# The projections' banks enter the scheduler's estimate, and the forget-gate decays reach the causal mask by accumulating DMA: a three-layer transformer kernel on one core

## The chip, the core and the metric

The kernel runs on one core of a Trainium2 chip. The metric is the time of one execution on the device, in microseconds (us). The engines are named as in the profile: PE is TensorE (matmuls, transposes), DVE VectorE, ACT ScalarE, POOL GpSimd, SP SyncE (it only issues transfers here). Each engine works through its own instructions strictly in program order and waits on semaphores for the others. SP and POOL also each own a queue of DMA transfers, which land asynchronously. DRAM is the device memory, SBUF the memory on the core, and a bank is one of eight accumulators of 128 x 512 f32 (PSUM) into which PE writes.

## What is computed

512 tokens of width 1024 go through three transformer layers in f32: block 1 once (block-sparse MoBA attention, gated linear attention GLA, a feed-forward network), then block 2 twice. The part of block 2 that the change touches, cut from the reference:

```python
log_f = jax.nn.log_sigmoid((f_logit + b_forget).astype(jnp.float32))
c = jnp.cumsum(log_f.astype(jnp.float32), axis=1).transpose(0, 2, 1)      # 8 heads
...
scores = jnp.einsum('bqhd,bkhd->bhqk', q_i, k).astype(jnp.float32) * scale
bias = c_i[..., :, None] - c[..., None, :]
causal = key_pos[None, :] <= q_pos[:, None]
logits = jnp.where(causal, scores + bias, -jnp.inf)
p = jax.nn.softmax(logits, axis=-1)
...
ret = retention_chunkwise(q_r, k_r, rv.reshape(rshape), gamma)
mixed = jnp.concatenate([fox_out.astype(x.dtype), ret_out], axis=-1)
x = layernorm(DEEPNORM_ALPHA * x + jnp.einsum('bsc,cd->bsd', mixed, w_out), ln1_g, ln1_b)
hid = jnp.square(jax.nn.relu(jnp.einsum('bsd,df->bsf', x, w_ff1)))
x = layernorm(DEEPNORM_ALPHA * x + jnp.einsum('bsf,fd->bsd', hid, w_ff2), ln2_g, ln2_b)
```

Attention has 8 heads of 64, handled as 4 pairs (pair 0 is heads 0 and 1, h0 and h1, and so on). Of the bias only the decay c at one of the two positions is added to the scores; the other is the same over a whole softmax row and drops out.

## The kernel before

**Precision.** Every f32 operand is split into a high and a low part in fp32r, and a product is three matmuls: high x high, low x high, high x low. Names with h or l at the end are the parts (wh, wl of a weight block; xTh, xTl of the activations; kh, kl of the keys).

**Weights.** A block of 512 KB is loaded by SP into `wr` (3 buffers), copied to `wh` by ACT (6 buffers), and DVE subtracts to get `wl`. The ACT copy waits until PE has finished with the block six back; SP's load waits for the DVE subtraction three back. All of this is issued in the order in which the program asks for blocks, mixed in each engine's queue with the attention's own work.

**Banks.** Four banks of tag "mm" take projections (`mm_ps`), four of tag "at" take everything else: scores, transposes, attention outputs (`at_ps`). Projections come in two forms. `proj_a` makes one 128-column slice for all tokens (24 matmuls into one bank): so q and k of each pair (q0, k0, ... q3, k3). `proj_b` takes all four mm banks for 512 columns: so the values. In block 2 the order is: values of attention, q0 k0 q1 k1 q2 k2 q3 k3, values of retention (a `proj_b`), then retention's own projections.

**Attention.** `attention_pair` turns the two banks of q and k into operands per head (ACT copies qs and kh, DVE makes the scaled qs and kl), which frees the banks. Then per head come the scores (8 matmuls in three banks), the softmax with its row maxima (DVE: instructions that add the bias, write ea, eb, ec and reduce; ACT: exponentials), transposes of the result (PE, tiles pta, ptb, ptc), and per pair the product with the values.

**What sets PE's order.** The program is a set of Python generators, threads, of which `Weave.run` advances one at a time while the kernel is built. Each instruction is charged to an estimate of its engine (`Engine.book`); `wv.now` is the estimated PE time. A thread that yields an event is not resumed before the event's estimated time, and one that yields a count is not resumed before that many "at" banks are free by the estimate (`banks`). So an estimate decides the order that every engine then follows, and a bad estimate costs a wait on the chip. The mm banks are not in it: a `proj_a` takes its bank at once, whether or not the chip will have freed it.

**The bias.** Block 2 writes the summed decays of the 8 heads to DRAM (`cd`). `fox_bias` loads one causal mask `tri` (128 x 512) per layer; per head SP loads that head's decays, the same 512 values for each of 128 partitions, into `row`, and POOL adds `cm` = `row` + `tri`. DVE uses `row` left of the diagonal blocks and `cm` on them. `row`, `tri` and `cm` come from a shared pool of 56 buffers of 256 KB.

Of the kernel before, what the change touches and what calls it, by code (L numbers as in the profile page):

```python
# [10 lines left out]
F32 = mybir.dt.float32  # L11
# [3 lines left out]
ALU = mybir.AluOpType  # L15
# [4 lines left out]
P, T, D = 128, 512, 1024  # L20
# [3 lines left out]
NM = 4  # L24
LAG = 0.6
SLACK = 0.0
HOLD = 1.5
BIG = 1.0e30
# [125 lines left out]
class Event:  # L154


    t = None


class Weave:  # L160
# [4 lines left out]
    def __init__(self, banks):  # L165
        self.now = self.chain = self.ready = 0.0
        self.threads, self.count = [], 0
        self.banks = {i: 0.0 for i in range(banks)}

    def spawn(self, gen, prio=1):  # L170
        self.count += 1
# [6 lines left out]
    def charge(self, eng, cost, args):  # L178
        self.chain = eng.book(self.chain, cost)
        self.ready = max(self.ready, self.chain)  # L180
        for a in args:
            n = getattr(getattr(a, "tensor", None), "name", None)
            if n in self.banks:
                self.banks[n] = max(self.banks[n], self.chain + HOLD)

    def bank(self, tile):

        del self.banks[min(self.banks, key=self.banks.get)]
        self.banks[tile.tensor.name] = self.now

    def mark(self, ev, more=0.0):
        ev.t = self.chain + LAG + more
# [75 lines left out]
def model_kernel(ctx: ExitStack, tc: tile.TileContext, I, out):  # L268
    nc = tc.nc
# [7 lines left out]
    psm = ctx.enter_context(tc.tile_pool(name="psm", bufs=NM, space=PSUM))  # L277
# [4 lines left out]
    wv = Weave(8 - NM)  # L282
    act, dve, pool = Engine(nc.scalar, wv, 0.2, 0.83), Engine(nc.vector, wv, 0.17, 1.04), Engine(nc.gpsimd, wv, 0.25, 2.1)
    uid = [0]

    def nm(s):
        uid[0] += 1
        return f"{s}_{uid[0]}"

    def bt(s="b", dt=F32):  # L290
        return pb.tile([P, T], dt, tag="b", name=nm(s))
# [7 lines left out]
        return pv.tile([P, 16], F32, tag="v", name=nm(s))  # L299

    def mm_ps():
        return psm.tile([P, T], F32, tag="mm", name=nm("mm"))

    def at_ps():
        t = psa.tile([P, T], F32, tag="at", name=nm("at"))
# [44 lines left out]
    def wblk(*key, pieces=1):  # L350
        key = key if len(key) == 7 else (*key, "")
        off, size = offs[key]
        nk = (key[3] - key[2]) // P
        raw = pw.tile([P, 1024], F32, tag="wr", name=nm("wr"), bufs=3)
        src = I["wall"][off : off + size].rearrange("(p w) -> p w", p=P)
        hi = pw.tile([P, 1024], F32R, tag="wh", name=nm("wh"))
        cuts = [slice(1024 // pieces * i, 1024 // pieces * (i + 1)) for i in range(pieces)]
        for c in cuts:
            with tc.issue_after(xdma[0].ins) if xdma else nullcontext():
                last_dma[0] = nc.sync.dma_start(raw[:, c], src[:, c])  # L360
            copy(hi[:, c], raw[:, c])
        if key[6]:
            h3 = hi.rearrange("p (k w) -> p k w", k=nk)
            r3 = raw.rearrange("p (k w) -> p k w", k=nk)
            sub_lo(h3[:, :, 32:64], r3[:, :, 32:64], h3[:, :, 32:64])
            return h3
        lo = pw.tile([P, 1024], F32R, tag="wl", name=nm("wl"))
        for c in cuts:
            sub_lo(lo[:, c], raw[:, c], hi[:, c])
        return hi.rearrange("p (k w) -> p k w", k=nk), lo.rearrange("p (k w) -> p k w", k=nk)  # L370
# [20 lines left out]
    def form_a(ps, w, c, acts, ks, toks=slice(0, T)):  # L391

        wh, wl = w
        n = len(ks)
        for i, k in enumerate(ks):
            h, l = acts.hs[k][:, toks], acts.ls[k][:, toks]
            mm(ps[:, toks], wh[:, i, c : c + P], h, i == 0, False)
            mm(ps[:, toks], wh[:, i, c : c + P], l, False, False)
            mm(ps[:, toks], wl[:, i, c : c + P], h, False, i == n - 1)
            yield 0  # L400
# [11 lines left out]
            yield 0  # L412

    def proj_a(name, l, c, acts, k=8):
        ps = mm_ps()
        yield from form_a(ps, wblk(name, l, 0, k * P, c, c + P), 0, acts, range(k))
        return ps

    def proj_b(name, l, k0, k1, c, acts, done, koff=0, tail=0, wait_k=False, wait_t=False, pre=None):
# [27 lines left out]
    def const(n):  # L447
        src = const_src(n)
        t = bt(n)[:, 0 : src.shape[1]]
        load(t, src)  # L450
        return t
# [48 lines left out]
    def row_bcast(src, n0):  # L500

        t = bt("row")
        load(t, bass.AP(tensor=src.tensor, offset=src.offset + n0, ap=[[0, P], [1, T]]))
        return t
# [686 lines left out]
        yield from block2(0, xw2, h)  # L1191


    def fox_bias(cd, tri):
        def bias(h):
            cb, cm = row_bcast(cd, T * h), bt("cm")
            pool.tensor_tensor(cm, cb, tri, ALU.add)

            def pieces(t):
                d = (P * t, P * t + P, cm[:, P * t : P * t + P])  # L1200
                return [d] if t == 0 else [(0, P * t, cb[:, 0 : P * t]), d]

            return pieces

        return bias
# [56 lines left out]
    def block2(l, xw, h):  # L1262
# [6 lines left out]
        dve.tensor_tensor_scan(a[0:8], one[0:8].to_broadcast([8, T]), f[0:8], 0.0, ALU.mult, ALU.add)  # L1269
        cd = pd.tile([8, T], F32, tag="cd", name=nm("cd"))  # L1270
        nc.sync.dma_start(cd, a[0:8])
        bias = fox_bias(cd, const("tri"))
        mix = Acts(8, "mix")
        for i in range(4):
            qk = []
# [16 lines left out]
        for i in range(4):  # L1292
            qk = []
            for j in range(2):
                ps = yield from proj_a("w_in_2", l, 1544 + 512 * j + P * i, xw)
# [9 lines left out]
        for i in range(4):  # L1305
            ps = yield from proj_a("w_in_2", l, 3080 + P * i, xw)
            ev, sg = sgs[i]
# [71 lines left out]
```

## Time and profile before

| quantity | value |
|---|---|
| time, median of 3 runs | 2039.48 us (2037.76 to 2041.69) |
| the profiled execution: time | 2039.07 us |
| its span (first to last instruction) | 2036.2 us |
| mean granted clock of PE, as a share of full speed | 0.993 |
| PE busy | 1990.4 us, 98% of the span |
| DVE, ACT, POOL busy | 56%, 47%, 16% |
| chain of work that ended last | 94% PE |

The span is the part of the time that the profile sees; 2.87 us of the profiled execution lie outside it. Idle time counts only on the engine that sets the end, and here that is PE. An idle stretch is shown in brackets behind the instruction that ended it, with the instruction that released it. The granted clock is what the chip's throttle let PE run at: 1.00 is 2.4 GHz and 0.50 is 1.2 GHz, the two levels; a value between is a mean over both.

### The profile page before, as it was taken

To read this page: it belongs to the slowest core of one execution; us is meant where nothing else is said; L and a number is where in the kernel's file an instruction comes from. 1 tells how busy PE (TensorE), PEld (TensorE's weight loads), DVE (VectorE), ACT (ScalarE), POOL (GpSimd) and SP (SyncE) were. 2 spreads that over 40 slices of the span, in tenths; PEclk is the share of its full clock that TensorE was granted. 3 is DMA by queue.
4 is the path that set the end of the run, shared out by engine and by line. 5 is a ranking of instruction groups with operands and counts; after the bars stand their busy time and mean duration, and the time that the engine had idled before them with its cause. 6 is when DMAs were issued, how large, how long until landed. Compare 5 with 4: busy or idle time off the path is not lost.

```text
span 2036.2 us, 25412 instructions
## 1 busy us (share of the span) xinstructions
PE 1990.4 (98%) x9478; PEld 1645.5 (81%) x9478; DVE 1148.5 (56%) x2028; ACT 954.0 (47%) x1663; POOL 319.1 (16%) x361
## 2 busy tenths in 40 slices
PE   8999899999999999999999999999999999999997
PEld 6777778888888888877888888888877888888886
DVE  6676444444566573475454656664675554656654
ACT  6566244333555453364333554552564334544551
POOL 2000110000212110010402201111211412211102
PEclk9999999999999999999999999999999999999999
DMA  5422112242766543332232745552422234666541
GB/s 200 156 91 76 52 63 93 94 154 73 181 158 137 154 126 114 100 108 80 81 125 92 167 144 130 150 149 79 140 84 87 69 115 142 138 159 157 131 133 42
DMA packets 93483, 240.49 MB, mean 118 GB/s; under 512 B 10734, under 2 KB 11200, under 8 KB 93360
## 3 DMA queue, kind: packets, MB, share of 16 engines
q1 hardware_dynamic: 72624, 201.12, 29.3%
q0 software_dynamic: 20736, 37.76, 11.6%
q8 instruction: 74, 1.21, 0.2%
q14 instruction: 49, 0.40, 0.1%
HBM read 236.69 MB, written 4.77 MB: 119 GB/s over the span
## 4 chain that ended last, share of the span: by engine, by line
PE 94%; ACT 2%; DVE 2%; POOL 1%; issue 1%; DMA 0%; SPq 0%; POOLq 0%; ACTq 0%; DVEq 0%
PE mm L311 67%; PE at L311 25%; PE at L320 3%; POOL h L262 1%; ACT wh L262 0%; ACT kh L262 0%; DMA xr<-in_xT_dram 0%; DVE og L262 0%; ACT qs L262 0%; DVE wl L262 0%; DVE qs L262 0%; ACT sil L262 0%; POOL mv L262 0%; ACT h L262 0%; POOL gm L262 0%
## 5 line engine op out<-in xcount | busy, mean ns | idle before, releaser
L262 DVE TENSOR_TENSOR wl<-wr,wh 128x1024 fp32r<-128x1024 f32 (+1 forms) x265 | 336.3, 1271 | 331.0 <-ACT wh L262 329.8
L262 ACT ACTIVATE wh<-wr 128x1024 fp32r<-128x1024 f32 (+1 forms) x268 | 282.5, 1056 | 474.4 <-PE mm L311 328.5
L262 DVE TENSOR_TENSOR wl<-sw,wh 128x512 fp32r<-128x512 f32 x252 | 166.0, 687 | 194.1 <-ACT wh L262 194.1
L262 ACT ACTIVATE wh<-sw 128x512 fp32r<-128x512 f32 x252 | 149.8, 626 | 224.9 <-PE at L311 121.6
L311 PE MATMUL at<-hTh,wh 128*128 128x512 f32 x576 | 224.1, 389 | 0.0
L311 PE MATMUL at<-hTl,wh 128*128 128x512 f32 x576 | 224.1, 389 | 0.0
L311 PE MATMUL at<-hTh,wl 128*128 128x512 f32 x576 | 224.1, 389 | 0.0
L669 POOL DMA_DIRECT2D sw<-in_wall_dram x144 | 127.3, 1051 | 606.7 <-DVE wl L262 450.1
L311 PE MATMUL mm<-xTh,wh 128*128 128x512 f32 x536 | 214.1, 399 | 0.0
L311 PE MATMUL mm<-xTl,wh 128*128 128x512 f32 x536 | 209.0, 390 | 0.0
L311 PE MATMUL mm<-xTh,wl 128*128 128x512 f32 x512 | 200.0, 391 | 0.0
L311 PE MATMUL mm<-wh,xl 128*128 128x512 f32 x504 | 196.2, 389 | 0.0
L311 PE MATMUL mm<-wl,xh 128*128 128x512 f32 x504 | 196.1, 389 | 0.0
L311 PE MATMUL mm<-wh,xh 128*128 128x512 f32 x504 | 196.1, 389 | 0.0
L311 PE MATMUL mm<-wh,xTh 128*128 128x512 f32 x352 | 146.2, 415 | 12.7 <-ACT wh L262 6.4
L311 PE MATMUL mm<-wl,xTh 128*128 128x512 f32 x352 | 140.0, 398 | 0.0
L311 PE MATMUL mm<-wh,xTl 128*128 128x512 f32 x352 | 139.7, 397 | 0.0
L311 PEld LDWEIGHTS at<-hTh,wh 128*128 128x128 f32 x576 | 108.2, 188 | 22.4
L311 PEld LDWEIGHTS at<-hTh,wl 128*128 128x128 f32 x576 | 108.1, 188 | 22.5
L311 PEld LDWEIGHTS at<-hTl,wh 128*128 128x128 f32 x576 | 108.1, 188 | 22.4
L311 PEld LDWEIGHTS mm<-xTh,wh 128*128 128x128 f32 x536 | 100.8, 188 | 19.6 <-ACT wh L262 0.5
L311 PEld LDWEIGHTS mm<-xTl,wh 128*128 128x128 f32 x536 | 100.9, 188 | 18.8
(287 smaller groups left out, 3809.6 us busy)
## 6 DMA issues: line engine op xcount, KB each, us to landing
wr<-in_wall_dram SPq DMA_DIRECT2D x266, 512.0 KB, 3.6
sw<-in_wall_dram SPq DMA_DIRECT2D x144, 256.0 KB, 5.8
sw<-in_wall_dram POOLq DMA_DIRECT2D x144, 256.0 KB, 6.0
row<-cd SPq DMA_DIRECT2D x16, 256.0 KB, 4.1
revp<-rev SPq DMA_DIRECT2D x1, 2560.0 KB
xr<-in_xT_dram SPq DMA_DIRECT2D x8, 256.0 KB, 6.1
g<-revp SPq DMA_DIRECT2D x8, 256.0 KB, 3.9
h<-in_x_dram SPq DMA_DIRECT2D x8, 256.0 KB, 5.9
```

The costliest lines, as they stand in the source:

```text
L262: return f(out, *a, **k)
L311: nc.tensor.matmul(out, lhsT, rhs, start=start, stop=stop, skip_group_check=more)
L320: nc.tensor.transpose(out, in_, ident)
L669: nc.gpsimd.dma_start(t, src, accum_op=ALU.add)
```

## The change

It has two parts. First, the estimate gets a second table, `mm`, for the four mm banks: a bank taken is marked as in use without end (BIG), and every charged instruction that touches it moves the time at which it comes free to its own end plus HOLD. `proj_a` now builds its weight block first, then yields `mm_free`, an event at the time when the first mm bank comes free by the estimate, and only then takes its bank. `proj_b` takes its four banks as before, with no yield. Second, `fox_bias` loads a fresh copy of `tri` for each head instead of one per layer, and adds the decays to it by a DMA on POOL's queue that accumulates into SBUF, straight from `cd`; the POOL addition and its charge in the estimate are gone. `row` is still loaded, for the blocks left of the diagonal.

```diff
     def __init__(self, banks):
 ...
         self.banks = {i: 0.0 for i in range(banks)}
+        self.mm = {i: 0.0 for i in range(NM)}
 ...
             if n in self.banks:
                 self.banks[n] = max(self.banks[n], self.chain + HOLD)
+            if n in self.mm:
+                self.mm[n] = self.chain + HOLD if self.mm[n] == BIG else max(self.mm[n], self.chain + HOLD)
 ...
+    def mm_bank(self, tile):
+
+        del self.mm[min(self.mm, key=self.mm.get)]
+        self.mm[tile.tensor.name] = BIG
+
+    def mm_free(self):
+
+        ev = Event()
+        t = min(self.mm.values())
+        ev.t = t if t < BIG else self.now
+        return ev
 ...
     def mm_ps():
-        return psm.tile([P, T], F32, tag="mm", name=nm("mm"))
+        t = psm.tile([P, T], F32, tag="mm", name=nm("mm"))
+        wv.mm_bank(t)
+        return t
 ...
     def proj_a(name, l, c, acts, k=8):
+        w = wblk(name, l, 0, k * P, c, c + P)
+        yield wv.mm_free()
         ps = mm_ps()
-        yield from form_a(ps, wblk(name, l, 0, k * P, c, c + P), 0, acts, range(k))
+        yield from form_a(ps, w, 0, acts, range(k))
         return ps
 ...
-    def fox_bias(cd, tri):
+    def fox_bias(cd):
         def bias(h):
-            cb, cm = row_bcast(cd, T * h), bt("cm")
-            pool.tensor_tensor(cm, cb, tri, ALU.add)
+            cb, cm = row_bcast(cd, T * h), const("tri")
+            nc.gpsimd.dma_start(cm, bass.AP(tensor=cd.tensor, offset=cd.offset + T * h, ap=[[0, P], [1, T]]), accum_op=ALU.add)
 ...
-        bias = fox_bias(cd, const("tri"))
+        bias = fox_bias(cd)
```

The number of instructions on PE, DVE, ACT and POOL stays the same; SP issues 14 more. The order differs in three stretches: block 1 from its attention to the end of GLA, and the attention of block 2 in each of its two layers (which change alike). Everything else, the feed-forward networks among it, is ordered as before.

**Block 2, layer 0, pair 3 on PE.** The names: `mm_1349` before and `mm_1367` after is the bank of k3; `mm_1372` before and `mm_1374` after is the first of the four banks of the `proj_b` behind it; `at<-kh,qs` are scores of head h4, in banks at_1368 and at_1370 before, at_1372 after. Before:

```order
L311 MATMUL at_1368_7328<-kh_1329_7166,qs_1328_7165 128x512
L311 MATMUL at_1368_7328<-kl_1330_7167,qs_1328_7165 128x512
L311 MATMUL at_1370_7337<-kh_1329_7166,qs_1328_7165 128x384
L311 MATMUL at_1370_7337<-kl_1330_7167,qs_1328_7165 128x384
L311 MATMUL mm_1349_7250<-xTh_736_3888,wh_1351_7252 128x512
L311 MATMUL mm_1349_7250<-xTl_738_3890,wh_1351_7252 128x512
L311 MATMUL mm_1349_7250<-xTh_736_3888,wl_1352_7255 128x512
```

After:

```order
L328 MATMUL mm_1367_7331<-xTh_737_3889,wh_1365_7326 128x512
L328 MATMUL mm_1367_7331<-xTl_739_3891,wh_1365_7326 128x512
L328 MATMUL mm_1367_7331<-xTh_737_3889,wl_1366_7329 128x512
L328 MATMUL at_1372_7365<-kh_1340_7220,qs_1339_7219 128x512
L328 MATMUL at_1372_7365<-kl_1341_7221,qs_1339_7219 128x512
L328 MATMUL mm_1367_7331<-xTh_737_3889,wh_1365_7326 128x512
L328 MATMUL mm_1367_7331<-xTl_739_3891,wh_1365_7326 128x512
L328 MATMUL mm_1367_7331<-xTh_737_3889,wl_1366_7329 128x512
L328 MATMUL mm_1374_7377<-wh_1379_7382,xTh_736_3888 128x512
L328 MATMUL mm_1374_7377<-wl_1380_7385,xTh_736_3888 128x512
L328 MATMUL mm_1374_7377<-wh_1379_7382,xTl_738_3890 128x512
```

Two banks of h4's scores stood ahead of 18 of k3's 24 matmuls; now the first stands among the last of them, and the rest come after matmuls of the `proj_b`.

**The same place on DVE.** `qs` and `kl` with a 64x512 tile are the operands of pair 3, which read the banks of q3 and k3 (`mm_1324`, `mm_1349` before; `mm_1338`, `mm_1367` after) and free them; the rows on `ea`, `eb` belong to h4's softmax. Before:

```order
L262 TENSOR_SCALAR ea_1340_7193<-ea_1340_7193,mx_1369_7331 128x512
L262 TENSOR_TENSOR wl_1479_7840<-wr_1477_7836,wh_1478_7837 128x1024
L262 RECIPROCAL mx_1371_7340<-mx_1371_7340 128x1
L262 COPY pta_1366_7326<-at_1379_7377 128x512
L262 TENSOR_SCALAR eb_1341_7194<-eb_1341_7194,mx_1371_7340 128x384
L262 SCALAR_TENSOR_TENSOR qs_1380_7383<-mm_1324_7155,qs_1380_7383 64x512
L262 TENSOR_TENSOR kl_1382_7385<-mm_1349_7250,kh_1381_7384 64x512
L262 SCALAR_TENSOR_TENSOR qs_1385_7396<-mm_1324_7155,qs_1385_7396 64x512
L262 TENSOR_TENSOR kl_1387_7398<-mm_1349_7250,kh_1386_7397 64x512
```

After:

```order
L277 ISA ea_1351_7249,mx_1373_7368<-at_1372_7365,row_1342_7228 128x384
L277 ISA mx_1373_7368 128x1
L277 SCALAR_TENSOR_TENSOR qs_1381_7390<-mm_1338_7215,qs_1381_7390 64x512
L277 ISA ea_1351_7249,mx_1373_7368<-at_1372_7365,tri_1343_7230,mx_1373_7368 128x128
L277 ISA mx_1373_7368 128x1
L277 TENSOR_TENSOR wl_1477_7845<-wr_1475_7841,wh_1476_7842 128x1024
L277 TENSOR_TENSOR kl_1383_7392<-mm_1367_7331,kh_1382_7391 64x512
L277 RECIPROCAL mx_1373_7368<-mx_1373_7368 128x1
L277 TENSOR_SCALAR ea_1351_7249<-ea_1351_7249,mx_1373_7368 128x512
L277 SCALAR_TENSOR_TENSOR qs_1386_7404<-mm_1338_7215,qs_1386_7404 64x512
L277 TENSOR_TENSOR kl_1388_7406<-mm_1367_7331,kh_1387_7405 64x512
```

The four operand rows stood behind all of h4's first reductions and a copy of transposes (`pta`); now only the reduction of h4's first bank stands among them.

**Block 1, pairs 2 and 3 on DVE.** `qs`, `kl` here are the operands of pair 2 and then of pair 3, from transposes in "at" banks; `ea_303<-at_327` (before `ea_302<-at_327`) is the first reduction of h4's scores, which frees the bank at_327. Before:

```order
L262 SCALAR_TENSOR_TENSOR qd_305_1428<-gqk_269_1290,qd_305_1428 128x512
L262 TENSOR_TENSOR ki_306_1429<-gqk_279_1341,ki_306_1429 128x512
L262 TENSOR_TENSOR yml_12_106<-at_309_1441,ymh_8_102 128x512
L262 SCALAR_TENSOR_TENSOR qs_315_1474<-at_313_1464,gains_97,qs_315_1474 64x512
L262 SCALAR_TENSOR_TENSOR kl_317_1476<-at_314_1465,gains_97,kh_316_1475 64x512
L262 SCALAR_TENSOR_TENSOR qs_319_1485<-at_313_1464,gains_97,qs_319_1485 64x512
L262 SCALAR_TENSOR_TENSOR kl_321_1487<-at_314_1465,gains_97,kh_320_1486 64x512
L262 ISA ea_302_1424,mx_328_1503<-at_327_1500,g_295_1409 128x512
```

After:

```order
L277 SCALAR_TENSOR_TENSOR qs_307_1441<-at_305_1431,gains_97,qs_307_1441 64x512
L277 SCALAR_TENSOR_TENSOR kl_309_1443<-at_306_1432,gains_97,kh_308_1442 64x512
L277 SCALAR_TENSOR_TENSOR qs_311_1452<-at_305_1431,gains_97,qs_311_1452 64x512
L277 SCALAR_TENSOR_TENSOR kl_313_1454<-at_306_1432,gains_97,kh_312_1453 64x512
L277 SCALAR_TENSOR_TENSOR qd_320_1469<-gqk_269_1290,qd_320_1469 128x512
L277 TENSOR_TENSOR ki_321_1470<-gqk_279_1341,ki_321_1470 128x512
L277 TENSOR_TENSOR wl_430_2017<-wr_428_2013,wh_429_2014 128x1024
L277 ISA ea_303_1429,mx_328_1509<-at_327_1506,g_296_1414 128x512
```

A weight subtraction (`wl_430`) now stands ahead of the reduction; it needs the ACT copy `wh_429`, which stands on ACT behind all operand copies of both pairs.

**Block 2, layer 0 on SP.** `cd` holds the decays, `wr` are weight blocks. Before:

```order
L360 DMA wr_1400_7458<-in_wall_dram 128x1024
L348 DMA row_1264_6900<-cd_1231_6799 128x512
L360 DMA wr_1423_7575<-in_wall_dram 128x1024
L348 DMA row_1269_6913<-cd_1231_6799 128x512
L360 DMA wr_1432_7629<-in_wall_dram 128x1024
L360 DMA wr_1467_7771<-in_wall_dram 128x1024
L348 DMA row_1299_7046<-cd_1231_6799 128x512
L348 DMA row_1304_7059<-cd_1231_6799 128x512
```

After:

```order
L365 DMA row_1263_6898<-cd_1231_6799 128x512
L365 DMA tri_1264_6900<-in_c128_dram 128x512
L377 DMA wr_1425_7590<-in_wall_dram 128x1024
L365 DMA row_1268_6912<-cd_1231_6799 128x512
L365 DMA tri_1269_6914<-in_c128_dram 128x512
L377 DMA wr_1449_7716<-in_wall_dram 128x1024
L377 DMA wr_1467_7788<-in_wall_dram 128x1024
L365 DMA row_1303_7064<-cd_1231_6799 128x512
L365 DMA tri_1304_7066<-in_c128_dram 128x512
L365 DMA row_1308_7078<-cd_1231_6799 128x512
L365 DMA tri_1309_7080<-in_c128_dram 128x512
```

Behind each `row` now stands a load of `tri`; on POOL each addition `cm<-row,tri` is replaced by a DMA `tri<-cd`, at the same place in its queue.

## Rows read from the trace of the kernel before

**Rows 1.** The page: busy time of the engines, and the chain that ended last

```profile
PE 1990.4 (98%) x9478; PEld 1645.5 (81%) x9478; DVE 1148.5 (56%) x2028; ACT 954.0 (47%) x1663; POOL 319.1 (16%) x361
...
PE 94%; ACT 2%; DVE 2%; POOL 1%; issue 1%; DMA 0%; SPq 0%; POOLq 0%; ACTq 0%; DVEq 0%
```

**Rows 2.** Waits of PE: for what, us in total, times, longest us

```profile
PE mm L311 <- DVE qs L262: 5.9, 2, 2.9
```

**Rows 3.** Timeline of PE, block 2 (idle before, releaser); both layers' attention

```profile
901.43 0.39 PE L311 MATMUL at<-kh,qs 128*128 128x256 f32 x1 [0.85 <-ACT pta L262]
...
918.57 0.49 PE L311 MATMUL mm<-wh,xTh 128*128 128x512 f32 x1 [2.94 <-DVE qs L262]
...
1517.36 0.79 PE L311 MATMUL mm<-wh,xTh 128*128 128x512 f32 x1 [2.94 <-DVE qs L262]
```

**Rows 4.** Stretches: length, busy us (instructions) of each engine, clock, DMA share, GB/s

```profile
918.50:922.00 3.50, 3.43 (x11) 2.72 (x12) 1.83 (x4) 1.07 (x2) 2.51 (x2) 0.61 0.02 9
922.00:926.00 4.00, 4.00 (x23) 3.25 (x22) 1.01 (x1) 2.42 (x4) 0.00 (x0) 0.91 0.00 0
1517.00:1521.00 4.00, 3.64 (x10) 2.86 (x11) 2.12 (x4) 1.32 (x3) 2.51 (x2) 0.50 0.10 35
1521.00:1525.00 4.00, 4.00 (x20) 3.25 (x18) 0.00 (x0) 1.68 (x3) 0.00 (x0) 0.69 0.00 0
220.00:224.00 4.00, 3.84 (x13) 3.15 (x14) 1.07 (x3) 0.19 (x1) 0.00 (x0) 0.63 0.00 0
250.00:260.00 10.00, 8.61 (x48) 6.92 (x48) 4.64 (x9) 2.51 (x4) 1.19 (x2) 1.00 0.29 91
```

**Rows 5.** Timeline of ACT, block 2, layer 0, pair 3

```profile
911.78 1.06 ACT L262 ACTIVATE wh<-wr 128x1024 fp32r<-128x1024 f32 x1 [0.43 <-PE mm L311]
...
913.35 0.57 ACT L262 ACTIVATE qs<-mm 64x512 fp32r<-64x512 f32 x1
```

**Rows 6.** Timeline of DVE, the same place

```profile
912.88 1.23 DVE L262 TENSOR_TENSOR wl<-wr,wh 128x1024 fp32r<-128x1024 f32 x1 [0.67 <-ACT wh L262]
...
917.82 0.69 DVE L262 SCALAR_TENSOR_TENSOR qs<-mm,qs 64x512 fp32r<-64x512 f32 x1 [1.30 <-ACT qs L262]
```

**Rows 7.** Tile row: count, ns min/median/max, first and last start; landing of its loads

```profile
L348 SPq DMA_DIRECT2D row<-cd x16: 370/384/427, 864.6 to 1513.8; - x16
L262 POOL TENSOR_TENSOR cm<-row,tri x16: 1274/1296/2256, 868.6 to 1518.9; 128x512 f32<-128x512 f32 x16
...
DMA to landing us min/median/max: 3.7/4.4/7.1
```

**Rows 8.** Timeline of DVE, first uses of cm: heads h0, h1, h2

```profile
876.39 0.34 DVE L262 CUSTOM_DVE_ANT_0 ea<-at,cm,mx 128x128 f32<-128x128 f32 x1
...
879.31 0.33 DVE L262 CUSTOM_DVE_ANT_0 ea<-at,cm,mx 128x128 f32<-128x128 f32 x1
...
902.87 0.35 DVE L262 CUSTOM_DVE_ANT_0 ea<-at,cm,mx 128x128 f32<-128x128 f32 x1
```

**Rows 9.** Timeline of SP's queue, loads of row for h0, h1, h2 and h3

```profile
864.63 0.37 SPq L348 DMA_DIRECT2D row<-cd  x1
...
869.45 0.42 SPq L348 DMA_DIRECT2D row<-cd  x1
...
882.45 0.90 SPq L348 DMA_DIRECT2D row<-cd  x2
```

**Rows 10.** Tile sw, weights of the FFNs: POOL's accumulating DMAs; landing of all

```profile
L669 POOL DMA_DIRECT2D sw<-in_wall_dram x144: 862/875/1870, 524.3 to 1936.0; - x144
...
DMA to landing us min/median/max: 3.6/5.9/10.1
```

**Rows 11.** Timeline of PE, block 1: the idle stretches where the order changes

```profile
158.90 0.36 PE L311 MATMUL at<-kh,qs 128*128 128x256 f32 x1 [1.94 <-DVE qs L262]
...
220.16 2.07 PE L311 MATMUL at<-v,kt 128*128 128x256 f32 x4 [4.13 <-DVE sta L262]
```

**Rows 12.** Timeline of ACT, block 1: the last operand copy of pair 3

```profile
160.15 0.63 ACT L262 ACTIVATE kl<-kl 64x512 fp32r<-64x512 f32 x1 [0.16 <-DVE kl L262]
```

## The prediction

> **What bounds the kernel now.** I read the page first: PE is busy for 98% of the span and makes up 94% of the chain that ended last [rows 1]. The work on PE is the same before and after, so only two things can move the time: PE's idle stretches, and the clock that PE is granted behind them. The view of PE's waits shows where a projection's bank was missing: two waits of 2.94 us, both on DVE's `qs` [rows 2]. The timeline places one in each layer of block 2. The stalled matmul is `mm<-wh,xTh`, which only a `proj_b` issues: it is the third of the four banks that the value projection of retention takes, and it was q3's. Another 0.85 us stands earlier in each layer, on a copy of transposes [rows 3].
>
> The windows show what a stall costs beyond itself. Behind the 2.94 us the clock is 0.61 for 3.5 us and 0.91 for 4 us in one layer, 0.50 and 0.69 for 4 us each in the other. Against 1.00 this loses 3.5 x 0.39 + 4 x 0.09 = 1.73 us and 4 x 0.50 + 4 x 0.31 = 3.24 us. The 4.13 us stall in block 1 has 0.63 for 4 us behind it, 1.48 us lost; an idle stretch of 1.39 us (inside 250 to 260 us) leaves the clock at 1.00 [rows 4]. So a short stall costs its length, a stall of 2.9 us or more costs 1.5 to 3.2 us on top. The Trainium skill, TensorE: Matmul & The Clock Gate, says that idle time on the engine drops its clock; these windows agree.
>
> Lost now in block 2's attention, per layer: 0.85 + 2.94 of stall, and 1.73 or 3.24 of clock: 5.5 and 7.0, together 12.5 us. This is what the change can win there.
>
> **Part one: the order, block 2.** After the change h4's scores follow most of k3's matmuls, so the operands of pair 3 no longer queue on DVE behind h4's softmax. Before, DVE reached the last `qs` of pair 3 at 917.82 us [rows 6], and PE stood until then. After, I chain by hand: k3's last matmuls end about 910.7; behind them ACT has a weight copy of 1.06 us and operand copies of 0.57 each [rows 5], DVE a `wl` of 1.23 and operand rows of 0.69 each [rows 6]. That puts the `qs` that frees q3's bank at 915.0 to 915.7. PE, with its shorter stalls, wants this bank at 914.5. So the wait does not vanish, since `proj_b` has no yield for its banks; it shrinks from 2.94 to about 1.25 us (0.5 to 2). The 0.85 us goes, because the copy of transposes now has projection matmuls between. I add 0.75 us for the biases (below) and 1 us for waits that I can't see, and take 3 us per layer, 2 at the least that I can chain. None is as long as 2.9 us, so the clock should stay. Gain in block 2: 12.5 - 2 x 3 = 6.5 us; 8.5 if only the chained 2 us remain.
>
> **Part one: block 1.** There the order moves too, though no projection waited for its mm bank. Gone are 0.19 + 1.94 = 2.13 us, of which the timeline shows the larger [rows 11]. But the transposes of pairs 2 and 3 now stand back to back, their operand copies fill ACT, and a weight copy stands behind them with DVE's `wl` in front of h4's first reduction. The last operand copy ended at 160.78 before [rows 12]; I place it at 160.5 after. Then `wh` (1.06), `wl` (1.23) and about 0.7 for the reduction give 163.4 for the bank at_327. PE wants it for h5's second score bank at about 160.1: the 158.90 of h4's third bank [rows 11] less 2.13 of stalls that are gone, plus the 3.3 us of matmuls that now stand between. The new stall is 3.3 us, long enough to cost clock (1.5 us); one of h7's transposes is late by about 1. In GLA 4.13 us of stall and 1.48 of clock stood before [rows 4, 11]; I chain several waits of up to 2.4 us in their place, in sum nearly as long, with the clock kept: 0.3 to 1.95 us less. Sum: -2.1 + 3.3 + 1.5 + 1 - 1.1 = +2.6 with the clock lost, +1.1 without. I have most doubt here, since no stall of exactly this kind stands in the trace; bounds -3 (the reduction isn't late) to +5 (stall and clock in full, GLA no better). I take +1, since the largest of these stalls rests on one ACT order that estimated times may place 1 us earlier.
>
> **Part two: the bias.** The 16 additions on POOL, 1.30 us each [rows 7], vanish; POOL is 16% busy, so they are worth nothing by themselves. What counts is when `cm` is there. Before: `row` lands 3.7 to 7.1 us after its issue, 4.4 in the middle [rows 7], then one addition. After: a `tri` load right behind `row`, which I price like `row`, then an accumulating DMA. The nearest rows for that are the FFN's accumulating weight loads on POOL's queue, of the same 256 KB: 0.88 us to issue; all loads of these tiles land 3.6 to 10.1 us after issue, 5.9 in the middle [rows 10]. They differ in the source (a weight block in DRAM there, here one row of 2 KB read for 128 partitions, as `row` itself is) and in the traffic beside them (busier there).
>
> Head h0: `row` is issued at 864.63 and `tri` 0.4 us behind [rows 9], there by 868.8; the sum lands between 872.4 and 878.9. DVE used `cm` first at 876.39 [rows 8], and wants it 6 matmuls, 1.36 us, earlier now: 875.0. At the middle it is in time, at the worst 3.9 late. Head h1: issue 869.45, `tri` there at 873.6, the sum at 877.2 to 883.7; wanted at 877.9 (879.31 less 1.36): 1.7 late at the middle, 5.8 at worst, of which some 2.9 is slack, since its transposes come at 887.5. Head h2: `row` at 882.45, sum at 890 to 897, wanted about 894 by my chain (902.87 before; its scores come earlier); 0.7 us of PE at the middle. Later heads have 3 us or more to spare. As `row`, with the same source pattern, lands in 4.4 us where the FFN's loads take 5.9, I take some 4.5 to 6, and 0.75 us per layer on PE. The 14 more loads of SP are 14 x 256 KB in stretches where the DMA engines are mostly idle (share 0.00 to 0.10 behind block 2's stalls, 0.29 in the row of block 1) [rows 4]; I price them at nothing. The accumulating DMA waits for `tri` on POOL's queue, and behind it there stand only other biases, which are wanted later.
>
> A rule against this part stands in the Trainium skill, SBUF — State Buffer, on DVE blocking DMA: some of DVE's operations shut POOL out of the port through which it writes descriptors, so that an issue is drawn out. The rows have 862 to 1870 ns for an issue beside the FFN's DVE work [rows 10], a drawing-out of 1 us at most; by it h1 would be 1 us later, inside the slack. The same skill, DMA: Bandwidth & Descriptors, Anatomy of one DMA, has a fit by which 256 KB on POOL's queue would take about 2.6 us (an estimate); by that no bias would be late, but the trace has nothing under 3.6.
>
> **Sum.** 2039.07 (the profiled execution, 0.4 below the median of three, which is nothing) - 6.5 + 1 = 2033.6 us.
>
> **The rivals.**
>
> A, the forecast: block 2's stalls shrink and lose their clock penalty, block 1 gives back a little. 2030 to 2036.
>
> B, stalls only change places. `proj_b` still meets q3's bank, and 1.25 us can be 2; the new block 1 stall costs its clock. Then block 2 keeps 4.5 us per layer (gain 12.5 - 9 = 3.5) and block 1 costs 3: 2038.5. For it: in pair 3 DVE's and ACT's operand rows follow each other with hardly a gap [rows 5, 6], so a stall removed at one place can come back at the next. Against it: the operands do move ahead of h4's softmax. To this belongs the case that the change does not do what it says: the only wait on a projection's bank that the trace has is in `proj_b`, which gets no yield.
>
> C, slower: the bias is late. If the accumulating DMA takes over about 7.5 us from issue to landing, h1 stalls PE by up to 2.9 us, h2 by up to 2.4, and with 1.25 at q3's bank and the clock lost once (1.7 to 3.2) a layer has about 9 us where it has 5.5 or 7.0 now: +5 to +6 over both, nothing from block 1's side: 2044. For it: the landing reaches 10.1 us and POOL's issue 1.87 [rows 10]. Against it: the traffic in this stretch is light, and `row` with the same source never takes more than 7.1.
>
> D, everything goes: 2 us per layer remain, block 1 gains 2 to 3. 2039 - 8.5 - 2.5 = 2028.
>
> **How the numbers follow.** A has 0.5, B 0.28, C 0.13, D 0.09. The measurement tells a change of 0.2%, 4.1 us, from none. A is faster by more than that in most of its range (2030 to 2035, nine tenths), D always, B never, C slower in nearly all, and B's worse end (block 1 at +5, 2041 and above) now and then. Faster 0.54, within 0.2% 0.30, slower 0.16. The range of 8 in 10 leaves out the best of D and the worst of C: 2027.5 to 2042.5. The likeliest alone: 2030 to 2036.
>
> **What would show it.** Right: PE's wait on `qs` in block 2 at 0.5 to 2 us in place of 2.94, with the clock at 1.00 behind it; no 0.85 on `pta`; a PE wait of about 3 us near 160 us, on DVE's `ea` or `mx`; DVE waiting at h1 on the accumulating DMA for under 3 us. Wrong: landings of `tri<-cd` over 7.5 us, with DVE and then PE waiting at h1 and h2 (C); a stall of 2.5 us or more at q3's bank, or the clock down in block 2 as before (B); no new stall in block 1 (D, or A with a larger gain).

## The result, and the profile after

The changed kernel is slower: 2053.37 us (median of 5 runs, 2050.66 to 2054.58) against 2038.86, a recorded ratio of 1.0064 with a 95% interval of 1.0052 to 1.0077 (the quotient of the two medians alone is 1.0071). The forecast was 2033.6 with a range of 2027.5 to 2042.5, so the time lies outside it, on the other side of no change. The profiled execution took 2053.37 us, its span is 2051.3.

The view of PE's waits in the changed kernel (what was waited for, us in total, times, longest us), beside [rows 2]:

```profile
PE at L337 <- DVE mixl L277: 10.8, 2, 5.4
PE at L328 <- DVE mx L277: 7.6, 5, 4.1
...
PE at L328 <- DVE sta L277: 4.3, 4, 1.7
...
PE mm L328 <- DVE qs L277: 1.9, 2, 1.0
```

The wait on `qs`, which was 2.94 us in each layer, is down to 0.96. A new one is larger: 5.4 us per layer on `mixl`. (Of the 7.6 us on `mx`, 4.1 are one wait in block 1.) `mixl` is the low part of a finished pair's attention output (`acts_out.split`): DVE makes it from the "at" bank into which PE wrote the product with the values, and this frees the bank. The timeline of PE in layer 0 and the windows behind the new wait and, last, behind the wait of block 1 (length, busy us of each engine, granted clock, DMA share, GB/s), beside [rows 3] and [rows 4]:

```profile
905.46 0.36 PE L328 MATMUL at<-kh,qs 128*128 128x256 f32 x1 [0.31 <-DVE mx L277]
912.27 0.48 PE L337 MATMUL at<-ident,eb 128*128 128x128 f32 x1 [5.40 <-DVE mixl L277]
930.57 0.50 PE L328 MATMUL mm<-wh,xTh 128*128 128x512 f32 x1 [0.96 <-DVE qs L277]
```

```profile
912.00:916.00 4.00, 3.73 (x11) 3.15 (x12) 3.96 (x22) 2.51 (x8) 0.86 (x1) 0.50 0.80 128
916.00:920.00 4.00, 4.00 (x14) 3.17 (x14) 0.53 (x3) 1.09 (x2) 0.00 (x0) 0.73 0.05 8
...
166.00:170.00 4.00, 3.11 (x9) 2.53 (x10) 3.91 (x20) 3.11 (x10) 0.00 (x0) 0.65 0.36 135
```

Where the 15.1 us of span went can be read from equal matmuls in both traces. Before 93 us, ahead of any change of order, the changed execution is already 1.2 us behind, lost in its first 14 us. Block 1 adds 3.6, up to 238 us. Layer 0 of block 2 adds 4.7 (the transposes behind its attention start at 1095.85, before at 1086.43) and layer 1 adds 4.4 (1700.22 against 1686.41); 1.3 are left for the rest. In layer 0 the waits make 6.9 us (0.26 more at 882 us) where they made 3.8, and the clock loses 4 x 0.50 + 4 x 0.27 = 3.1 us where it lost 1.73: +4.5.

### The profile page after: what moved, and what is told of

It is laid out like the page before. It is cut to its first block, busy times and chain, and to the rows that moved or that the text cites. A ratio compares the mean times of both kernels' runs of the same rounds, so it can differ in the third digit from the quotient of the medians.

```text
span 2051.3 us, 25433 instructions
## 1 busy us (share of the span) xinstructions
PE 1994.2 (97%) x9478; PEld 1647.0 (80%) x9478; DVE 1146.0 (56%) x2028; ACT 956.3 (47%) x1663; POOL 309.1 (15%) x361
## 4 chain that ended last, share of the span: by engine, by line
PE 88%; DVE 3%; DMA 3%; ACT 3%; POOL 1%; issue 1%; SPq 0%; POOLq 0%; ACTq 0%; DVEq 0%
PE mm L328 63%; PE at L328 22%; PE at L337 2%; DMA sw<-in_wall_dram 1%; DMA tri<-cd 1%; POOL h L277 1%; DVE wl L277 1%; DMA tri<-in_c_dram 1%; ACT wh L277 0%; ACT kh L277 0%; DVE qs L277 0%; ACT kl L277 0%; ACT qs L277 0%; DVE kl L277 0%; DMA xr<-in_xT_dram 0%
```

## The experiments

All times are medians, with the recorded ratio to the kernel before on the same chip and its 95% interval; the ratio isn't the quotient of the two medians alone.

| run | what it is | us | ratio (interval) |
|---|---|---|---|
| e1 | mm table alone | 2040.62 | 1.0009 (1.0001 to 1.0017) |
| e2 | POOL's addition uncharged, alone | 2045.89 | 1.0030 (1.0018 to 1.0042) |
| e3 | accumulating DMA alone, charge kept | 2037.40 | 0.9994 (0.9986 to 1.0003) |
| e4 | e1 and e2 together | 2045.71 | 1.0034 (1.0023 to 1.0045) |
| e5 | changed kernel, charge put back | 2039.69 | 1.0012 (1.0003 to 1.0021) |
| e6 | changed kernel, masks early | 2038.29 | 1.0003 (0.9994 to 1.0012) |
| e7 | e3, and proj_b yields | 2039.68 | 1.0006 (0.9997 to 1.0015) |
| e8 | e2, pair 2's operands after pair 0's mix | 2027.16 | 0.9949 (0.9937 to 0.9962) |
| e9 | changed kernel with e8's order of pair 2 | 2038.52 | 1.0003 (0.9994 to 1.0011) |
| e10 | e8 with early masks and accumulating DMA | 2029.39 | 0.9961 (0.9949 to 0.9973) |
| e11 | e6, masks loaded again per head | 2038.50 | 1.0000 (0.9991 to 1.0009) |
| e12 | e6's order, POOL's addition | 2038.78 | 0.9997 (0.9988 to 1.0006) |
| e13 | e6's order, bias late | 2041.70 | 1.0015 (1.0006 to 1.0024) |
| e14 | changed kernel's order, bias in time | 2045.57 | 1.0031 (1.0020 to 1.0043) |

### Which of the three parts

The change turned out to have three parts, not two, since the new bias also drops a charge from the estimate. Two theories stood against each other. LATE: the bias arrives late by DMA. ORDER: the new order of block 2 makes PE wait whatever the bias does.

e1, the table and `proj_a`'s yield with the bias as before:

> The table of mm banks and the yield in proj_a alone; the bias is made as before (one tri per layer, POOL adds, and the addition is charged to the estimate). In the instruction lists PE's order then differs from before only in block 1, and is there that of the changed kernel. If block 1's loss of some 3.6 us in the changed kernel is this order's, as its 4.09 us wait near 167 us says: 2038.9 + 3.6 = 2042.5 us, with block 2 as before (waits of 0.85 and 2.94 us in each layer). If the table also works for block 2, as the forecast had it, the 2.94 us is shorter and the time is 2036 to 2039.

e2, the kernel before with one word changed:

```diff
-            pool.tensor_tensor(cm, cb, tri, ALU.add)
+            nc.gpsimd.tensor_tensor(cm, cb, tri, ALU.add)
```

> The kernel before, with POOL's addition of the bias still done but no longer charged to the estimate; no table of mm banks, no new DMA. In the instruction lists PE's order is then that of before in block 1 and that of the changed kernel in block 2. Theory LATE (the bias that arrives late by DMA makes block 2's loss; the new order is good): no wait of 5.4 us, q3's bank about 1 us, no clock lost, about 6 us saved: 2033. Theory ORDER (the new order puts pair 0's mixl behind pair 2's operands, and PE waits for it whatever the bias does): a wait on mixl of 2.5 us or more in each layer, and its clock: 2038 to 2043.

e3, the kernel before with the new bias, and the charge of the addition kept:

```diff
-            cb, cm = row_bcast(cd, T * h), bt("cm")
-            pool.tensor_tensor(cm, cb, tri, ALU.add)
+            cb, cm = row_bcast(cd, T * h), const("tri")
+            wv.charge(pool, pool.fixed + pool.per * T / 1000.0, (cm, cb))
+            nc.gpsimd.dma_start(cm, bass.AP(tensor=cd.tensor, offset=cd.offset + T * h, ap=[[0, P], [1, T]]), accum_op=ALU.add)
```

> The accumulating DMA and the tri loads per head alone, with POOL's addition still charged to the estimate though it is no longer there, so that PE's order is that of before throughout; no table of mm banks. LATE: DVE waits for tri<-cd at h0 to h2 as in the changed kernel, PE stalls behind it, 3 to 4.5 us more per layer than before: 2045 to 2048. ORDER: DVE's waits are mostly absorbed, 0 to 1 us per layer: 2039 to 2041.

e4, the changed kernel with e2's line for the bias:

> The changed kernel's order in full (table of mm banks, POOL's addition not charged), but the bias made as before by one tri per layer and POOL's addition. PE's order is that of the changed kernel throughout. LATE: block 1's +3.6 and block 2's gain of 6: 2036 to 2037. ORDER: block 2's loss stays for the most part: 2042 to 2050. If the three parts are independent, the time is that of before plus the differences of the table alone and of the uncharged addition alone.

e5, the changed kernel with e3's `wv.charge` line added:

> The changed kernel with one thing put back: the estimate charges POOL 1.1 us or so per head again, though the addition is now a DMA. In the instruction lists PE's order is then that of before in block 2 and that of the changed kernel in block 1. If the dropped charge, through the order of block 2, is what costs, the time is that of the mm table alone less what the DMA bias saves: 2040.6 - 0.6 = 2040. If the mm table or the DMA in themselves cost more than the runs so far showed: 2045 or more.

The instruction lists settle what the table does: it moves PE's work in block 1 alone. Block 2's whole new order on PE comes from the dropped charge (e2). e5 confirms it on the chip: with the charge back, the changed kernel is 2039.69, within 1 us of e1 and 13.7 under the change. The table costs 0.1% (e1); its profile has the 4.08 us wait of block 1 and in block 2 the old 0.86 and 2.94. The uncharged order costs 0.3% (e2, e4). The accumulating DMA in PE's old order costs nothing (e3): DVE waits 2.56 us for h1's sum there, and PE doesn't feel it. It isn't the DMA quite alone: by the traces ACT's and DVE's orders between the first heads moved in e3 too, and the 0.85 us on `pta` is gone, which may hide a small loss. But the parts don't add up: with the DMA the new order is 7.7 us slower than without it (2053.4 against 2045.7), in PE's old order it is not slower at all.

### What stands behind the wait on mixl

In e2 the wait on `mixl` is 3.73 us, with the bias as before. The chain of e2 up to that wait (start, length, what):

```profile
898.63 0.70 DVE qs L262
...
899.77 0.59 DVE kl L262
900.36 0.02 issue
900.39 0.63 ACT kl L262
901.02 0.03 issue
901.04 0.60 ACT qs L262
901.64 0.02 issue
901.67 0.69 DVE qs L262
902.36 0.03 issue
902.39 0.70 DVE kl L262
903.10 0.02 issue
903.12 0.63 ACT kl L262
903.75 0.03 issue
903.77 0.61 ACT mixh L262
904.38 0.02 issue
904.40 0.70 DVE mixl L262
```

PE had finished pair 0's product with the values by 899.2. The split of it, `mixh` on ACT and `mixl` on DVE, stands in both queues behind pair 2's operands, which go to and fro between ACT and DVE for 5 us. h2's transposes (h3's in the expectation of e8) need a bank, and the next to come free is the one that `mixl` frees.

Before, pair 2's operands stood ahead of this split too, but long ahead of it. DVE's first and last operand row of pair 2 and the split, in the kernel before and then in the changed one:

```profile
892.12 0.68 DVE L262 SCALAR_TENSOR_TENSOR qs<-mm,qs 64x512 fp32r<-64x512 f32 x1
...
897.67 0.69 DVE L262 TENSOR_TENSOR kl<-mm,kh 64x512 fp32r<-64x512 f32 x1
...
906.50 0.68 DVE L262 TENSOR_TENSOR mixl<-at,mixh 128x512 fp32r<-128x512 f32 x1
```

```profile
905.75 0.68 DVE L277 SCALAR_TENSOR_TENSOR qs<-mm,qs 64x512 fp32r<-64x512 f32 x1
...
909.51 0.69 DVE L277 TENSOR_TENSOR kl<-mm,kh 64x512 fp32r<-64x512 f32 x1
...
911.52 0.69 DVE L277 TENSOR_TENSOR mixl<-at,mixh 128x512 fp32r<-128x512 f32 x1 [1.32 <-ACT mixh L277]
```

Before, the operands were done 8 us ahead of the split, and PE asked for the bank only at 912.50, behind h4's first scores and 21 matmuls of projections. In the changed kernel PE ends pair 0's product at 904.1, before the first of these operand rows starts, and asks for the bank at 906.87, three matmuls behind h3's scores. The new order makes the operands and the split fall due together. e8 takes this apart:

```diff
                 def get():
+                    if i == 2:
+                        yield mix.ev[0]
                     return q, k, -0.125, None
```

> The kernel before with POOL's addition uncharged (e2), but pair 2's operands may not be made before the estimate has pair 0's mix split, so that mixh and mixl stand ahead of pair 2's operands on ACT and DVE. PE's order is the same up to the transposes of h3. If the 3.73 us wait on mixl in e2 is the queue behind those operands, it goes (under 0.5 us), and 4 to 6 us per layer come back unless pair 2's later operands make a new wait: 2034 to 2041. If the wait has another cause it stays near 3.7 us, and the time at 2045 or above.

The wait is gone, the one on q3's bank too (PE's order behind h2's first transposes moves as well, so this second gain isn't the split's alone), and e8 is the fastest kernel of the study, 0.5% under the kernel before. PE's timeline of layer 0's attention in e8 has one idle stretch left, and the windows show the clock kept:

```profile
920.30 0.36 PE L311 MATMUL at<-kh,qs 128*128 128x256 f32 x1 [0.45 <-DVE mx L262]
```

```profile
900.00:910.00 10.00, 10.00 (x53) 8.24 (x52) 8.86 (x30) 7.67 (x16) 1.29 (x1) 1.00 0.21 69
910.00:920.00 10.00, 9.85 (x54) 6.80 (x52) 6.90 (x22) 7.84 (x16) 2.55 (x2) 1.00 0.28 93
920.00:930.00 10.00, 9.70 (x49) 8.15 (x50) 9.41 (x38) 5.66 (x17) 1.29 (x1) 1.00 0.24 78
```

The same line in the changed kernel, and in the changed kernel without `proj_a`'s yield and with all eight masks of a layer loaded ahead of its value projection:

> The changed kernel with pair 2's operands made only after pair 0's mix is split (as in e8), nothing else changed: the bias still comes from tri loaded per head and the accumulating DMA, the mm table still orders block 1. If the two causes found (late bias, operands queued ahead of mixl) each matter by themselves, the wait on mixl shrinks from 5.4 us to about what h2's late bias alone makes (2 to 3 us), block 1 keeps its 2 to 3.6: 2036 to 2042. If the queue ahead of mixl was the only way in which the late bias reached PE, block 2 comes out as in e8: 2027.2 + 2 to 3 = 2029 to 2031.

> e8's order of PE throughout (block 1 as before, block 2 with the uncharged bias and pair 2's operands after pair 0's mix), with the bias by eight early tri loads and the accumulating DMA in place of POOL's addition. If the accumulating DMA is worth something where the masks are there in time, 0 to 2 us under e8: 2025 to 2027. If it costs anything by itself (POOL's queue, more transfers ahead of the layer): 2028 or more.

e9 gives back 14.9 us. It keeps block 1's loss, and in block 2 waits of 0.98 and 1.57 us on `mx` that e8 doesn't have; where every microsecond of the rest of its distance to e8 lies wasn't followed. e10 is no faster than e8: their intervals overlap, and the accumulating DMA wins nothing over POOL's addition.

### Late bias or ACT's order

In the changed kernel DVE does wait for the sums. The waits of POOL's and DVE's work on one of them, h2's, in the chain of the changed kernel:

```profile
889.03 1.23 DVE wl L277
...
890.66 0.43 SPq L365
891.09 0.05 issue
891.14 5.05 DMA tri<-in_c_dram
...
896.21 0.04 POOLq L1216
896.25 0.47 issue
896.72 5.49 DMA tri<-cd
...
902.25 0.09 issue
902.34 0.34 DVE ea L277
```

`row` and `tri` stand on SP behind a load of weights that waits for DVE's `wl` at 889.03; then two transfers of 5 us follow each other. e6 loads the masks early:

```diff
     def block2(l, xw, h):
         fv = []
+        tris = [const("tri") for _ in range(8)]
...
-            cb, cm = row_bcast(cd, T * h), const("tri")
+            cb, cm = row_bcast(cd, T * h), tris[h]
```

> The changed kernel, PE's and DVE's order unchanged, but the eight tri tiles of a layer are loaded ahead of its value projection, so that the accumulating DMA no longer waits for a mask loaded just before it. If the 7 to 8 us between the new order with POOL's addition (2045.7) and the changed kernel (2053.4) come from row, tri and accumulation standing in series behind SP's weight loads, DVE's waits for tri<-cd go and the time falls to 2045 to 2047. If the accumulation itself (5.2 us from issue to landing) is what is late, or the accumulating transfers slow others, it stays at 2051 to 2053.

It gives back all 15 us, more than the bias in time can explain by e4. The reason is a second difference: ACT's order moved too. In the changed kernel ACT's copy `kl` of one head stands ahead of `qs` of the next, here behind it, so that ACT needn't wait for DVE between the heads. Two runs meant to part the two:

e11 loads each mask a second time (`load(cm, const_src("tri"))`) behind `row`; e12 replaces the DMA of e6 by `nc.gpsimd.tensor_tensor(cm, cb, cm, ALU.add)`.

> e6 with its bias made late again: the masks are loaded early as in e6, and each is loaded a second time right behind row, as in the changed kernel, ahead of the accumulation. Early loads also moved six of ACT's operand copies per layer by one place in e6; here ACT's order is that of e6, PE's that of the changed kernel, so only the arrival of the bias differs from e6. If e6's gain of 15 us was the bias in time, the time goes back to 2049 to 2053 with waits for tri<-cd of over 2 us and some 5 us on mixl. If it was ACT's order, it stays at 2038 to 2040; if both, it lies between, about 2045.

> e6 with POOL adding row to the early mask in place of the accumulating DMA; the instruction lists of PE, DVE and ACT are those of e6 throughout. If ACT's order makes the difference between e4 (2045.7, POOL's addition) and e6 (2038.3), this is 2038 to 2040. If the accumulating DMA with early masks is what is faster than row plus addition, it stays near e4, 2044 to 2046.

e11 failed as a test: its second loads were issued early, the accumulations of layer 0 are all issued from 868 us on, and nothing is late. e12 shows ACT's order at work without any DMA in the bias: 2038.78 against e4's 2045.71, with PE's order the same. Two more runs give the missing corners. e13 makes each accumulation of e6 wait for `row`; e14 puts an unused `const("tri")` at the place where the change loads its mask, which brings back the changed kernel's order on ACT, while the sums go onto early masks:

```diff
+            nc.gpsimd.tensor_scalar(cm[:, 0:1], cb[:, 0:1], 0.0, None, ALU.mult)     # e13
+            const("tri")                                                              # e14
```

> In e11 the second loads of the masks were issued early, so the bias was in time after all and e11 repeated e6. Here the orders of PE, DVE and ACT are those of e6, the masks are early, but POOL first writes one column of the mask from row (times zero, so the sum is unchanged), and the accumulation behind it can't start before row has landed. Row and tri land together in the changed kernel, so the sums arrive about when they do there. If the late bias makes block 2's loss: waits for tri<-cd of 1 to 2.5 us on DVE, some 5 us on mixl, 2046 to 2053. If ACT's order makes it: 2038 to 2041, with the waits absorbed.

> The other corner: PE, DVE and ACT are ordered exactly as in the changed kernel, all its loads of tri are still made (unused), but the accumulation goes onto masks loaded ahead of the layer, so that the bias is in time. If the late bias makes block 2's loss: 2038 to 2041, the wait on mixl about 2 us as in e6. If ACT's order makes it (each head's kl copy ahead of the next head's qs): the wait on mixl 3.5 to 4 us, 2044 to 2047 as in e4. If both are needed for 2053, this and the run with the late bias in e6's order both lie well under it.

| time (wait on mixl in layers 0 and 1) | bias in time | bias late |
|---|---|---|
| ACT's kl behind the next qs | e6: 2038.29 (2.15, 2.14) | e13: 2041.70 (3.81, 2.70) |
| ACT's kl ahead of the next qs | e14: 2045.57 (3.73, 3.73) | changed kernel: 2053.37 (5.40, 5.39) |

In these four runs PE's and DVE's orders are one, and ACT's is one along each row of the table. Both causes matter: ACT's order is worth 7.3 us with the bias in time and 11.7 with it late, the late bias 3.4 and 7.8. (The medians of the kernel before that were taken beside these runs lie between 2038.0 and 2039.3, so that each of these figures has about 1 us of doubt.)

That each cause matters more beside the other is not shown, since e13's bias is not always as late as the changed kernel's. DVE's first use of h2's sum in layers 0 and 1, in the changed kernel and then in e13:

```profile
902.34 0.35 DVE L277 CUSTOM_DVE_ANT_0 ea<-at,tri,mx 128x128 f32<-128x128 f32 x1 [2.46 <-DMA tri<-cd]
...
1506.88 0.35 DVE L277 CUSTOM_DVE_ANT_0 ea<-at,tri,mx 128x128 f32<-128x128 f32 x1 [3.52 <-DMA tri<-cd]
```

```profile
901.75 0.35 DVE L277 CUSTOM_DVE_ANT_0 ea<-at,tri,mx 128x128 f32<-128x128 f32 x1 [2.58 <-DMA tri<-cd]
...
1500.15 0.35 DVE L277 CUSTOM_DVE_ANT_0 ea<-at,tri,mx 128x128 f32<-128x128 f32 x1 [0.79 <-DMA tri<-cd]
```

In layer 0, where the sum is about equally late, the effects add up: PE's wait on `mixl` is 1.66 and 1.67 us longer with the bias late, 1.58 and 1.59 longer with ACT's other order, and all its waits in the attention make 2.4 us in e6, 4.5 in e13, 4.7 in e14 and 6.9 in the changed kernel. In layer 1 they make 2.4, 3.0, 4.7 and 7.7. The time rises by three to five and a half times the mean rise of a layer's wait on `mixl`: there are two layers, and behind the wait others, and in part the loss by the clock, grow with it. Why a load of a mask between the heads moves ACT's copies when the kernel is built stays open.

### The yield that proj_b lacks

e7 is e3 with the table, no yield in `proj_a`, and in `proj_b` of block 2:

```diff
-        pss = [mm_ps() for _ in range(NT)]
+        pss = []
...
             for t in range(NT):
+                if len(pss) < NT:
+                    if name == "w_in_2":
+                        yield wv.mm_free()
+                    pss.append(mm_ps())
```

> A version meant to be faster: DMA bias with POOL's charge kept, the table of mm banks, no yield in proj_a, but proj_b in block 2 takes its four banks one at a time and yields for each. Block 1 is ordered as before; in block 2 ten rows of transposes, scores and values now stand between the second and the third bank of the value projection of retention. If the missing yield in proj_b is what leaves the 2.94 us wait on q3's bank, that wait falls under 1 us, its clock is kept, and 4 to 5.5 us are saved per layer: 2028 to 2031. If the wait only moves (to the transposes or to another bank): 2035 to 2039.

The wait on q3's bank is gone, and the gain is nothing, since a wait of 3.29 us on a copy of transposes has taken its place:

```profile
921.54 0.48 PE L337 MATMUL at<-ident,eb 128*128 128x128 f32 x1 [3.29 <-DVE ptb L277]
```

`ptb` stands on DVE behind pair 3's operand rows (`qs` at 919.35, `kl` at 920.07, `ptb` at 920.80): it is the same queue as that ahead of `mixl`.

## Why the prediction was wrong

**Block 2's order, the step that failed.** "After the change h4's scores follow most of k3's matmuls, so the operands of pair 3 no longer queue on DVE behind h4's softmax" was right, and so was the size that followed: q3's bank was late by 0.96 us (forecast 1.25, 0.5 to 2), and the 0.85 on `pta` went. What failed is a sentence behind it: "I add 0.75 us for the biases (below) and 1 us for waits that I can't see". The wait that wasn't seen is 5.4 us, on `mixl`. The operands of pair 2 had moved too, to directly ahead of pair 0's split, and I followed only the pair at which the old wait stood. With it fell "None is as long as 2.9 us, so the clock should stay": the windows have 0.50 and 0.73. The rule behind that sentence, "a stall of 2.9 us or more costs 1.5 to 3.2 us on top", rested on three stalls of one trace, and doesn't hold either way (last section). Rival B had the form of it, a stall that changes its place, but looked for it in block 1 and at q3's bank.

**What made that order.** The forecast gave block 2's order to the mm table, and held it against the change that `proj_b` got no yield. The table does nothing there; the charge that went with POOL's addition does (e2, e5). "They are worth nothing by themselves" was said of the additions' time on POOL, and holds; their charge in the estimate, though, 0.25 + 2.1 x 0.512 = 1.33 us each (not the 1.1 of e5's expectation), was worth 6 to 8 us of order. And the yield for `proj_b`, tried in the old order, doesn't help (e7).

**The bias.** The term of the sum was "0.75 us for the biases" in each layer; between e14 and the changed kernel, which are ordered alike, the late bias is worth 7.8 us over both. The sums' own transfers were priced well: the landings of tile `tri`, loads and sums together, are 3.9, 5.3 and 6.6 us (shortest, middle, longest; forecast 4.5 to 6). The load of `tri` ahead of the sum was not: it was placed 4.2 us behind `row`'s issue (868.8 less 864.63), and for h2 it lands 5.5 us behind (891.14 + 5.05, less 890.66). In PE's old order nothing is lost (e3). In layer 0 h0 and h1 are 1.16 and 1.09 us late on DVE. The step that failed is h2's, late on DVE by 2.46 and 3.52 us in the two layers, where I had 0.7 us of PE: I took `row`'s issue from [rows 9], 882.45, and it came at 890.66. The whole execution is 4.7 us behind by then; the other 3.5 come about because the weight load ahead of it on SP waits for a `wl` that comes later on DVE: it stands later in the order, and behind the waits for h0's and h1's sums. Rival C's condition, a landing over 7.5 us, never occurred; its direction came true all the same, by SP's queue. The estimate of 2.6 us for a sum, from the fit of the Trainium skill, DMA: Bandwidth & Descriptors, Anatomy of one DMA, doesn't hold here: the middle of the 16 sums is 5.2 us. ("The trace has nothing under 3.6" is true of the rows that the prediction shows; SP's weight loads of 512 KB land from 3.3 us on.) The drawing-out of issues, from the Trainium skill, SBUF — State Buffer, on DVE blocking DMA, doesn't show in the changed kernel: the 16 issues of `tri<-cd` took 853 to 934 ns. In e6, where the eight sums of a layer are issued one upon the other, the issues took 862 to 3276 ns; no run shows why.

**Block 1.** The mechanism was right and the stall mis-sized: 4.09 us on the reduction behind `wl`, forecast 3.3. `wl` took 2.01 us in place of 1.23, beside POOL work, and ACT's copies, with one of GLA's (`ki`) behind the last operand's, ended at 163.1 where I had 160.5 (1.2 us of this is the lag from the start). The sum was put at +1, with +2.6 if the clock fell; it fell (0.65 for 4 us), and the profile has +3.6. Timed alone it is +0.2 to +3.5 (e1).

## What to carry to other kernels

Where an estimate orders the work, a cost removed from the estimate is a change of order, and has to be read as one: taken apart, a one-word edit that leaves the work as it was cost about half of the loss (6 to 8 of 14.5 us). When a stall goes, follow every shared buffer that the moved instructions now stand ahead of, on every in-order engine, and not only the one that was late before; here both new waits were small splits and copies behind another pair's operands. When an experiment gives back more than its cause can explain, compare the orders on all engines before believing it.

## What the runs showed of the hardware

The clock behind equal stalls isn't equal. Behind the 2.94 us on `qs` the kernel before lost 1.73 and 3.24 us [rows 4]; in the profiled execution of e1 the same wait stands twice, and the clock stays:

```profile
922.30:926.30 4.00, 3.98 (x23) 3.31 (x23) 1.71 (x3) 1.84 (x4) 2.54 (x2) 1.00 0.02 9
1519.30:1523.30 4.00, 3.99 (x23) 3.32 (x24) 1.70 (x3) 1.85 (x4) 2.53 (x2) 1.00 0.05 17
```

Nor does the length decide between a loss and none. In block 1 a wait of 1.94 us on `qs` stands alike in the kernel before and in e3 (1.95 there), and behind it the clock stays at 1.00 in the one and is down in the other; behind the 2.15 us on `mixl` in e6 it is down too. The kernel before, e3, e6:

```profile
158.90:162.90 4.00, 4.00 (x20) 3.39 (x21) 3.41 (x13) 3.71 (x10) 0.00 (x0) 1.00 0.00 0
```

```profile
160.76:164.76 4.00, 4.00 (x14) 3.24 (x15) 3.42 (x13) 3.70 (x10) 0.00 (x0) 0.62 0.00 0
```

```profile
907.00:911.00 4.00, 4.00 (x14) 3.21 (x15) 3.93 (x23) 2.51 (x8) 0.00 (x0) 0.63 0.02 4
```

The profiled execution of e1 took 2037.46 us, near the fastest of e1's twelve (2037.35 to 2042.82, median 2040.62), with a mean clock of 0.996 where those above 2041 us have 0.992 to 0.994. That of e2 took 2040.57, 5.3 us under e2's median of 2045.89, with 0.993 against 0.990 or 0.991. A single profile can thus be 3 to 5 us off its kernel's median, it seems mostly by the clock, and a sum that takes the clock's loss from one profile has that much doubt in it.
